# Last expert layer of a fused two-block kernel: gathers, weight places and the overflow count arranged anew

## The chip, the cores and the metric

The kernel runs on one core of a Trainium2 chip. Its time is the device time of one execution in microseconds (us), and the median of several executions is given. One of them is recorded by the hardware profiler; all rows below come from that execution. PE is the matrix engine (TensorE), DVE the vector engine, ACT the scalar engine, SP the engine whose queue issues all the large weight transfers here.

## The reference

Two transformer blocks run one after the other on 256 tokens of 1024 numbers, in float32. The last part of the second block is a mixture of eight experts; each token goes to two of them:

```python
def _moe_swiglu(h, w_router, w_gate, w_up, w_down):
    logits = (h @ w_router).astype(jnp.float32)
    top_vals, top_idx = lax.top_k(logits, TOP_K)
    top_w = jax.nn.softmax(top_vals, axis=-1)
    gates = jnp.sum(jax.nn.one_hot(top_idx, N_EXPERTS, dtype=jnp.float32) * top_w[..., None], axis=-2)
    out = jnp.zeros_like(h)
    for e in range(N_EXPERTS):
        y = _swiglu(h, w_gate[e], w_up[e], w_down[e])
        out = out + gates[..., e:e + 1].astype(h.dtype) * y
    return out
```

`_swiglu` is silu(h W_gate) times (h W_up), multiplied by W_down. The inner width FF is 3584, so each expert has three matrices of 1024 x 3584 numbers, 44 MB, and all eight are read from memory: 352 MB. `h` is the RMS-normalised residual; the block adds `out` to it.

## The kernel before, in words

`moe2` is the last stage of the program, from about 1107 us to the end. It works on routed tokens only.

- **Choice.** `logits` (L685) transposes the residual x, multiplies it by the router, and picks two experts for each token. It also splits all of x into two parts, `th` (ACT, L300) and `tl` (DVE, L137), each in fp32r, a rounded float32 form. A number is then the sum of its two parts.
- **Places.** The experts are ranked by how many tokens they have. Place 0 is expert 0; the rest follow by count. Places 0 to 4 are large, with 128 slots for tokens, 5 to 7 small, with 64. They run in the order `SEQ = (0, 5, 1, 2, 6, 3, 4, 7)`. A token beyond an expert's slots is an overflow: `beyond` (L723) counts those, with a chain on DVE, a transpose on PE (L735) and a read of the number by SP (L928), after which a second pass runs if the number is not zero.
- **Gathers.** The tokens of an expert are brought together by a product with a one-hot matrix. `gather(p, k)` does this for one of eight blocks of 128 rows: four fp32r products, `th` and `tl` times two halves of the tokens, then ACT and DVE split the result. `gather_small` does it for all three small experts at once, 192 columns wide. The eight gathers of place 0 stand ahead of everything; `some()` sets the others, one behind each step of a down product of the expert ahead: the small gathers in place 0, those of 1 in 5, of 2 in 1, of 3 in 6, of 4 in 3.
- **Weights.** Each expert has 42 weights of 1 MB: 28 for gate and up, in seven chunks of 512 columns (the loop over `c`), and 14 for down. In a large expert `slab` (L266) loads a weight into one of five `raw` tiles (DMA at L270). ACT copies each half of it to fp32r (L277) and DVE subtracts (L137); the two parts go to one of seven `wx` tiles. Three products per block follow (`mm3`): six records of 512 columns for each half of a weight. In a small expert `whole` (L261) loads the weight (L1456 gate and up, L1592 down) and PE uses it in plain float32, without splitting. It takes the five `raw` and then the seven `wx` tiles in rotation, by a counter that runs through the whole program.
- **Order.** PE follows the written order in this stage (`manual_schedule`). The other engines are ordered by the scheduler. SP issues the weight transfers one after the other, and each waits there until its tile is free.
- The work on the tables by places (`by_place`, `one_hot`, the shares) and the overflow count stand in the loop at `p == 0 and c == 1`; in chunk 2 each expert multiplies its slots by the gate.

Of the kernel before, what the change touches and what calls it, by code (L numbers as in the profile page):

```python
# [19 lines left out]
P = 128  # L20
D = 1024
# [32 lines left out]
    "moe2": dict(t8=3, t4=0, t2=5, t1=3, t0=4, tz=16, hh=7, hl=7),  # L54
# [15 lines left out]
class Fused:  # L70
    def __init__(self, ctx, tc, A):
# [7 lines left out]
        self.fences, self.holds, self.wholes = [], [], -1  # L79
# [181 lines left out]
    def whole(self, *shape):  # L261

        n, self.wholes = sum(WBUFS.values()), self.wholes + 1
        tag = "raw" if self.wholes % n < WBUFS["raw"] else "wx"
        return self.wp.tile([P, *shape], F32, name=self.name("whole"), tag=tag, bufs=WBUFS[tag])

    def slab(self, src, k, n):
        nc = self.nc
        raw = self.wp.tile([P, k, n], F32, name=self.name("raw"), tag="raw", bufs=WBUFS["raw"])
# [415 lines left out]
    def logits(self, x, w, choose, bias=None):  # L685

        th, tl = self.T([P, 2, D], F32R), self.T([P, 2, D], F32R)
# [3 lines left out]
        def half(t, c):  # L691
            self.split(th[:, t, c:c + 512], tl[:, t, c:c + 512], x[:, t, c:c + 512])
# [671 lines left out]
    def moe2(self, x, out):  # L1364
# [5 lines left out]
        names = "l1_moe_w_gate_2", "l1_moe_w_up_2", "l1_moe_w_down_2"  # L1370
        lg, rank, chosen = self.T([P, 2, 8]), self.T([P, 2, 8]), self.T([P, 2, 8], BF)
# [5 lines left out]
        raw, th, tl = self.logits(x, self.rt2_w, choose)  # L1377
# [28 lines left out]
        def gather(p, k):  # L1406
# [6 lines left out]
            for i, q in enumerate((th, tl)):  # L1413
                for t in range(2):
                    self.mm(ps, q[:, t, k * P:(k + 1) * P], oh[:, t, p], i == 0 and t == 0, i == 1 and t == 1)
# [5 lines left out]
        def gather_small(p, k):  # L1421
# [4 lines left out]
            for i, q in enumerate((th, tl)):  # L1426
                for t in range(2):
                    self.mm(ps, q[:, t, k * P:(k + 1) * P], oh[:, t, p:E, 0:CAP1], i == 0 and t == 0, i == 1 and t == 1)
# [74 lines left out]
        for at, p in enumerate(SEQ):  # L1503
            hids, small = [], p >= SMALL
            first, final = at == 0, at == E - 1
            ahead = SEQ[at + 1] if not final else p
            ahead = iter([] if final or ahead > SMALL else
                         [(gather_small if ahead == SMALL else gather, (ahead, k)) for k in range(8)])

            def some():  # L1510
                for f, args in ahead:
                    f(*args)
                    break
# [8 lines left out]
            for c in range(FF // 512):  # L1522
                hid = self.T([P, 512])
                if small:
# [3 lines left out]
                    later.append((turn_small, (hid, hids)))  # L1528
                else:
# [8 lines left out]
                if p == 0 and c == 1:  # L1538
# [37 lines left out]
                    over, cnt = self.beyond(slot, shares, None, E)  # L1576
# [116 lines left out]
```

## Time and profile before

| | before |
|---|---|
| median of 3 runs | 2085.85 us (2085.8 to 2087.02) |
| profiled execution | 2086.38 us, span 2084.6 us |
| granted TensorE clock, mean | 0.987 |
| PE busy | 1980.3 us (95%) |
| DVE busy | 1201.8 us (58%) |
| ACT busy | 989.9 us (47%) |
| moved by DMA | 576.46 MB, mean 277 GB/s |

The span is what the recorded instructions cover; the execution's own time is 1.8 us longer. Busy shares are means over the whole program, which has several stages; the last one is about 47% of it. A window row shows the time from and to, its length, then for PE, PEld (weight loads), DVE, ACT and POOL the busy time with the number of instructions, then the granted clock (1.00 is 2.4 GHz), the busy share of the DMA engines and the GB/s that they moved. In a timeline a row is a start, a length and an instruction, or several alike in a row; behind it in brackets stands the idle time before it and what ended that. A wait on a "DMA" is one for a transfer to land.

### The profile page before, as it was taken

To read this page: it belongs to the slowest core of one execution; us is meant where nothing else is said; L and a number is where in the kernel's file an instruction comes from. 1 tells how busy PE (TensorE), PEld (TensorE's weight loads), DVE (VectorE), ACT (ScalarE), POOL (GpSimd) and SP (SyncE) were. 2 spreads that over 40 slices of the span, in tenths; PEclk is the share of its full clock that TensorE was granted. 3 is DMA by queue.
4 is the path that set the end of the run, shared out by engine and by line. 5 is a ranking of instruction groups with operands and counts; after the bars stand their busy time and mean duration, and the time that the engine had idled before them with its cause. 6 is when DMAs were issued, how large, how long until landed. Compare 5 with 4: busy or idle time off the path is not lost. (4 is left out here: it accounts for less than half of the span.)

```text
span 2084.6 us, 27119 instructions
## 1 busy us (share of the span) xinstructions
PE 1980.3 (95%) x10288; PEld 1411.8 (68%) x10288; DVE 1201.8 (58%) x1853; ACT 989.9 (47%) x1469; POOL 42.4 (2%) x66
## 2 busy tenths in 40 slices
PE   7999998999989999999998999899999889999987
PEld 7977445875437979987776883378877237887722
DVE  6856116643146656656778860189886018988600
ACT  4564123632236444444566861177675117767510
POOL 2000000000000000000000000000000000000000
PEclk9999998999999999999999999999999999999999
DMA  9337995547976446555335999999999999999998
GB/s 265 125 104 243 331 368 187 181 154 272 366 285 227 142 142 202 183 168 198 122 117 204 319 351 386 402 348 353 342 349 332 387 402 371 358 342 342 376 387 330
DMA packets 327411, 576.46 MB, mean 277 GB/s; under 512 B 11738, under 2 KB 124088, under 8 KB 327144
## 3 DMA queue, kind: packets, MB, share of 16 engines
q1 hardware_dynamic: 324808, 568.33, 78.1%
q0 software_dynamic: 2464, 6.31, 1.1%
q8 instruction: 83, 1.36, 0.3%
q14 instruction: 56, 0.46, 0.1%
HBM read 573.55 MB, written 1.05 MB: 276 GB/s over the span
## 5 line engine op out<-in xcount | busy, mean ns | idle before, releaser
L137 DVE TENSOR_TENSOR wx<-raw,wx 128x1024 fp32r<-128x1024 f32 (+3 forms) x642 | 752.7, 1210 | 172.9 <-ACT wx L277 167.2
L277 ACT CAST wx<-raw 128x1024 fp32r<-128x1024 f32 (+3 forms) x642 | 641.0, 1043 | 202.2 <-PE acc L149 144.2
L149 PE MATMUL ms<-wx,hl 128*128 128x512 f32 x1960 | 515.7, 396 | 5.0 <-ACT wx L277 2.7
L149 PEld LDWEIGHTS ms<-wx,hl 128*128 128x128 f32 x1960 | 364.6, 189 | 93.2 <-DVE wx L137 14.4
L149 PE MATMUL acc<-hl,wx 128*128 128x256 f32 x2112 | 273.5, 288 | 2.7 <-ACT wx L277 1.6
L149 PEld LDWEIGHTS acc<-hl,wx 128*128 128x128 f32 x2112 | 261.8, 194 | 5.7 <-ACT wx L277 2.1
L149 PE MATMUL ms<-whole,xg 128*64 128x512 f32 x672 | 177.4, 600 | 24.7 <-DMA whole<-in_l_moe_w_up_dram 24.6
L134 ACT ACTIVATE t<-ms,tz 128x512 f32<-128x512 f32 (+4 forms) x101 | 60.5, 602 | 290.8 <-PE ms L149 281.6
L149 PE MATMUL acc<-wx,hl 128*128 128x512 f32 (+1 forms) x720 | 180.3, 403 | 4.7 <-DVE wx L137 3.1
L149 PE MATMUL ms<-wx,hh 128*128 128x512 f32 x560 | 176.4, 395 | 1.5 <-DVE wx L137 1.5
L146 DVE SCALAR_TENSOR_TENSOR t<-ms,tz,t 128x512 f32<-128x512 f32 (+2 forms) x69 | 51.8, 750 | 214.6 <-ACT t L134 174.8
L149 PE MATMUL acc<-wx,t 128*128 128x512 f32 (+1 forms) x732 | 174.0, 394 | 0.5 <-DVE t L1038 0.5
L149 PEld LDWEIGHTS acc<-wx,hl 128*128 128x128 f32 x720 | 135.1, 193 | 35.7 <-DVE wx L137 3.6
L149 PEld LDWEIGHTS acc<-wx,t 128*128 128x128 f32 x732 | 135.2, 188 | 29.9 <-DVE t L1038 0.9
L149 PEld LDWEIGHTS ms<-whole,xg 128*64 128x64 f32 x672 | 52.2, 136 | 128.4 <-issue 73.2
L149 PEld LDWEIGHTS ms<-wx,hh 128*128 128x128 f32 x560 | 103.5, 188 | 25.0 <-DVE wx L137 3.8
L149 PE MATMUL ms<-whole,hl 128*64 128x512 f32 x512 | 117.0, 598 | 0.5 <-DVE t L137 0.5
L149 PE MATMUL ms<-whole,hh 128*64 128x512 f32 x336 | 83.5, 604 | 12.4 <-DMA whole<-in_l_moe_w_down_dram 12.3
L149 PEld LDWEIGHTS tp<-t,t 128*128 128x128 f32 (+1 forms) x432 | 57.3, 185 | 49.5 <-issue 32.4
L146 DVE SCALAR_TENSOR_TENSOR t<-tp,tz,t 128x512 fp32r<-128x512 f32 x32 | 23.9, 747 | 95.5 <-ACT t L134 95.5
L149 PEld LDWEIGHTS ms<-whole,hl 128*64 128x64 f32 x512 | 35.0, 136 | 60.1 <-issue 55.8
L149 PE MATMUL tp<-t,t 128*128 128x256 f32 (+4 forms) x432 | 72.1, 294 | 1.6 <-DVE t L137 1.6
(275 smaller groups left out, 1544.4 us busy)
## 6 DMA issues: line engine op xcount, KB each, us to landing
raw<-in_l_moe_w_gate_dram SPq DMA_DIRECT2D x70, 1024.0 KB, 7.2
raw<-in_l_moe_w_up_dram SPq DMA_DIRECT2D x70, 1024.0 KB, 7.2
raw<-in_l_moe_w_down_dram SPq DMA_DIRECT2D x70, 1024.0 KB, 7.6
whole<-in_l_moe_w_gate_dram SPq DMA_DIRECT2D x42, 1024.0 KB, 14.1
whole<-in_l_moe_w_up_dram SPq DMA_DIRECT2D x42, 1024.0 KB, 14.2
whole<-in_l_moe_w_down_dram SPq DMA_DIRECT2D x42, 1024.0 KB, 18.3
whole<-in_moe_w_gate_dram SPq DMA_DIRECT2D x64, 512.0 KB, 8.2
whole<-in_moe_w_up_dram SPq DMA_DIRECT2D x64, 512.0 KB, 8.8
```

Source lines behind the costliest of these rows:

```text
L134: return self.nc.scalar.activation(out, in_, func, **kw)
L137: return self.nc.vector.tensor_tensor(out, a, b, op=op)
L146: return self.nc.vector.scalar_tensor_tensor(out, a, s, b, op0=op0, op1=op1, **kw)
L149: return self.nc.tensor.matmul(out, lhsT, rhs, start=start, stop=stop, **kw)
L277: nc.scalar.copy(h, raw[:, a:a + m])
```

## The change

Four things change in `moe2`:

- The two parts `th`, `tl` of x are not made; gathers multiply plain float32 x by the one-hot matrix, two products in place of four.
- The two tiles that this sets free become places for weights (`more=2`). `slab` rotates over seven tiles instead of five, `whole` over fourteen (five, two, seven) instead of twelve, and both counters start anew at this layer.
- The gathers are spread differently: those of places 1 and 2 lie in the small expert 5, those of 3 and 4 in 6, from the sixth chunk on and then behind each down step; the small gathers stay in place 0; the large experts 1 to 4 have none.
- `beyond` stands at chunk 4 of place 0 instead of chunk 1.

```diff
--- before.py
+++ after.py
@@ -51,7 +51,7 @@
     "sg": dict(t8=6, t4=2, t2=4, t1=1, t0=3, tz=8),
     "ffn": dict(t8=7, t4=0, t2=4, t1=1, t0=1, tz=16),
     "diff": dict(t8=0, t4=7, t2=8, t1=4, t0=8, tz=24, hd=8, acc=3, av=1),
-    "moe2": dict(t8=3, t4=0, t2=5, t1=3, t0=4, tz=16, hh=7, hl=7),
+    "moe2": dict(t8=1, t4=0, t2=5, t1=3, t0=4, tz=16, hh=7, hl=7, more=2),
 }
 
 
@@ -76,7 +76,7 @@
         self.wp = ctx.enter_context(tc.tile_pool(name="weights", bufs=1))
         self.hp = ctx.enter_context(tc.tile_pool(name="inputs", bufs=1))
         self.n = 0
-        self.fences, self.holds, self.wholes = [], [], -1
+        self.fences, self.holds, self.wholes, self.raws = [], [], -1, -1
         self.x = self.X()
         for t in range(2):
             self.nc.sync.dma_start(self.x[:, t], A["x"][0, t * P:(t + 1) * P])
@@ -260,13 +260,24 @@
 
     def whole(self, *shape):
 
-        n, self.wholes = sum(WBUFS.values()), self.wholes + 1
-        tag = "raw" if self.wholes % n < WBUFS["raw"] else "wx"
-        return self.wp.tile([P, *shape], F32, name=self.name("whole"), tag=tag, bufs=WBUFS[tag])
+        more = self.bufs.get("more", 0)
+        n, self.wholes = sum(WBUFS.values()) + more, self.wholes + 1
+        if self.wholes % n < WBUFS["raw"]:
+            tag = "raw"
+        else:
+            tag = "more" if self.wholes % n < WBUFS["raw"] + more else "wx"
+        return self.piece("whole", [P, *shape], tag)
+
+    def piece(self, name, shape, tag):
+        if tag == "more":
+            return self.ap.tile(shape, F32, name=self.name(name), tag=tag, bufs=self.bufs[tag])
+        return self.wp.tile(shape, F32, name=self.name(name), tag=tag, bufs=WBUFS[tag])
 
     def slab(self, src, k, n):
         nc = self.nc
-        raw = self.wp.tile([P, k, n], F32, name=self.name("raw"), tag="raw", bufs=WBUFS["raw"])
+        self.raws += 1
+        at = self.raws % (WBUFS["raw"] + self.bufs.get("more", 0))
+        raw = self.piece("raw", [P, k, n], "raw" if at < WBUFS["raw"] else "more")
         nc.sync.dma_start(raw, src)
         m = k // SPLIT if k % SPLIT == 0 else k
         hs, ls = [], []
@@ -682,14 +693,15 @@
             at += w.shape[1]
         return wc
 
-    def logits(self, x, w, choose, bias=None):
-
-        th, tl = self.T([P, 2, D], F32R), self.T([P, 2, D], F32R)
+    def logits(self, x, w, choose, bias=None, parts=True):
+
+        th, tl = (self.T([P, 2, D], F32R) if parts else None for _ in range(2))
         n = w.shape[2]
         out, xT = self.T([P, 2, n]), self.HL([P, 8, S], F32)
 
         def half(t, c):
-            self.split(th[:, t, c:c + 512], tl[:, t, c:c + 512], x[:, t, c:c + 512])
+            if parts:
+                self.split(th[:, t, c:c + 512], tl[:, t, c:c + 512], x[:, t, c:c + 512])
 
         for t in range(2):
             s = slice(t * P, (t + 1) * P)
@@ -1368,13 +1380,14 @@
         nc, A = self.nc, self.A
         E, FF = 8, 3584
         names = "l1_moe_w_gate_2", "l1_moe_w_up_2", "l1_moe_w_down_2"
+        self.wholes = self.raws = -1
         lg, rank, chosen = self.T([P, 2, 8]), self.T([P, 2, 8]), self.T([P, 2, 8], BF)
 
         def choose(t, lg):
             self.ranks(rank[:, t:t + 1], lg[:, None], 1, 8)
             self.ts(chosen[:, t], rank[:, t], 1.5, None, OP.is_lt)
 
-        raw, th, tl = self.logits(x, self.rt2_w, choose)
+        raw, _, _ = self.logits(x, self.rt2_w, choose, parts=False)
         rx = self.token_scale(x)
         found, slot = self.places(chosen, E, True), self.T([P, 2, E])
         oh = self.T([P, 2, E, CAP2], F32R)
@@ -1410,9 +1423,8 @@
                 inputs[p] = xp[:, 0], xp[:, 1]
             xH, xL = inputs[p]
             ps = self.PS([P, CAP2], "ms" if p == 0 and k % 2 else "tp")
-            for i, q in enumerate((th, tl)):
-                for t in range(2):
-                    self.mm(ps, q[:, t, k * P:(k + 1) * P], oh[:, t, p], i == 0 and t == 0, i == 1 and t == 1)
+            for t in range(2):
+                self.mm(ps, x[:, t, k * P:(k + 1) * P], ohf[:, t, p], t == 0, t == 1)
             last = self.split(xH[:, k], xL[:, k], ps, self.gcol("l1_moe", k))
             if p == 0:
                 self.awake(psr[3], WG)
@@ -1423,9 +1435,8 @@
             if k == 0:
                 inputs[p] = self.xp.tile([P, 8, E - p, CAP1], F32, name=self.name("xg"), tag="x")
             ps = self.PS([P, E - p, CAP1], "tp")
-            for i, q in enumerate((th, tl)):
-                for t in range(2):
-                    self.mm(ps, q[:, t, k * P:(k + 1) * P], oh[:, t, p:E, 0:CAP1], i == 0 and t == 0, i == 1 and t == 1)
+            for t in range(2):
+                self.mm(ps, x[:, t, k * P:(k + 1) * P], ohf[:, t, p:E, 0:CAP1], t == 0, t == 1)
             self.act(inputs[p][:, k], ps, AF.Copy, scale=self.gcol("l1_moe", k))
 
         def source(p, i, k0, nk, c0, n):
@@ -1503,9 +1514,8 @@
         for at, p in enumerate(SEQ):
             hids, small = [], p >= SMALL
             first, final = at == 0, at == E - 1
-            ahead = SEQ[at + 1] if not final else p
-            ahead = iter([] if final or ahead > SMALL else
-                         [(gather_small if ahead == SMALL else gather, (ahead, k)) for k in range(8)])
+            after = [q for q in SEQ[at + 1:at + 3] if q < SMALL] if small else SEQ[at + 1:at + 2] if first else []
+            ahead = iter([(gather_small if q == SMALL else gather, (q, k)) for q in after for k in range(8)])
 
             def some():
                 for f, args in ahead:
@@ -1526,6 +1536,8 @@
                     self.act(hid[64:128], ps[0:64], AF.Silu, scale=scol[0:64])
                     self.stt(hid[64:128], ps[64:128], scol[64:128], hid[64:128], OP.mult, OP.mult)
                     later.append((turn_small, (hid, hids)))
+                    if c > 4:
+                        some()
                 else:
                     g = up(p, c, 0)
                     catch_up()
@@ -1573,7 +1585,9 @@
                     self.ts(room, place[:, 0], SMALL - 0.5, float(CAP2 - CAP1), OP.is_lt, OP.mult)
                     self.ts(room, room, 1000.0 + CAP1 - 0.5, None, OP.add)
                     self.tt(slot, slot, room[:, None].to_broadcast([P, 2, E]), OP.subtract)
-                    over, cnt = self.beyond(slot, shares, None, E)
+                    spare = slot, shares
+                if p == 0 and c == 4:
+                    over, cnt = self.beyond(*spare, None, E)
                 if c == 2:
                     psg = self.PS([P, 1], "tp")
                     for t in range(2):
```

On PE, in expert 0, the transpose of the count (L735, after L747) stands between weights. Before, where `ms_10100` is the up product of chunk 1, `wx` are halves of weights and `hl` the gathered tokens:

```order
L149 MATMUL ms_10100<-wx_10123,hl_9901 128x512 x6
L149 MATMUL ms_10100<-wx_10126,hl_9901 128x512 x6
L735 MATMUL ms_10190<-c_78,tz_10188 1x128
L149 MATMUL ms_10197<-wx_10200,hl_9901 128x512 x6
L149 MATMUL ms_10197<-wx_10203,hl_9901 128x512 x6
L149 MATMUL ms_10197<-wx_10221,hl_9901 128x512 x6
L149 MATMUL ms_10197<-wx_10224,hl_9901 128x512 x6
L1468 MATMUL tp_10239<-c_78,t_1713_10047 128x128 x4
```

In the changed kernel, in the up product of chunk 4 and what follows:

```order
L149 MATMUL ms_10411<-wx_10434,hl_9891 128x512 x6
L149 MATMUL ms_10411<-wx_10437,hl_9891 128x512 x6
L747 MATMUL ms_10456<-c_78,tz_10454 1x128
L149 MATMUL ms_10463<-wx_10466,hl_9891 128x512 x6
L149 MATMUL ms_10463<-wx_10469,hl_9891 128x512 x6
L149 MATMUL ms_10463<-wx_10487,hl_9891 128x512 x6
L149 MATMUL ms_10463<-wx_10490,hl_9891 128x512 x6
L1479 MATMUL tp_10505<-c_78,t_1785_10358 128x128 x4
```

The transpose has moved down by twelve weights; before it stood ahead of chunk 2, now it stands ahead of chunk 5.

On SP, the first weights of the second small expert, place 6, and what each waits for. Before:

```order
L1456 DMA whole_13489<-in_l_moe_w_gate_dram 128x4x512 [waits DVE_49,PE_49]
...
L1456 DMA whole_13491<-in_l_moe_w_up_dram 128x4x512 [waits DVE_49,PE_49]
...
L1456 DMA whole_13501<-in_l_moe_w_gate_dram 128x4x512 [waits DVE_49,PE_49]
...
L1456 DMA whole_13503<-in_l_moe_w_up_dram 128x4x512 [waits DMAHW6_49,DVE_49,PE_49]
...
L1456 DMA whole_13521<-in_l_moe_w_gate_dram 128x4x512 [waits DMAHW7_49,DVE_49,PE_49]
...
L1456 DMA whole_13523<-in_l_moe_w_up_dram 128x4x512 [waits DMAHW0_49,DVE_49,PE_49]
```

In the changed kernel (the rows between them are register instructions):

```order
L1467 DMA whole_13415<-in_l_moe_w_gate_dram 128x4x512 [waits DMAHW4_49,DVE_49]
...
L1467 DMA whole_13417<-in_l_moe_w_up_dram 128x4x512 [waits DMAHW5_49,DVE_49]
...
L1467 DMA whole_13427<-in_l_moe_w_gate_dram 128x4x512 [waits DMAHW6_49,DVE_49]
...
L1467 DMA whole_13429<-in_l_moe_w_up_dram 128x4x512 [waits DMAHW7_49,DVE_49]
...
L1467 DMA whole_13447<-in_l_moe_w_gate_dram 128x4x512 [waits DMAHW0_49,DVE_49]
...
L1467 DMA whole_13449<-in_l_moe_w_up_dram 128x4x512 [waits DMAHW1_49,DVE_49]
```

Before, the first transfers go to tiles that PE has to leave; now they go to tiles that DVE has to leave.

On PE, in the small expert of place 5, the changed kernel has a gather between chunks 5 and 6, where `x_9633` is the residual itself:

```order
L149 MATMUL ms_11185<-whole_11198,xg_10672 64x512
L149 MATMUL ms_11185<-whole_11200,xg_10672 64x512
L149 MATMUL tp_11220<-t_1679_9861,x_9633 128x128 x2
L149 MATMUL ms_11226<-whole_11227,xg_10672 64x512
L149 MATMUL ms_11226<-whole_11229,xg_10672 64x512
```

It is two products of the program; before, a gather was four.

## Rows read from the trace of the kernel before

**Rows 1.** Windows by expert, places 0, 5, 1, 2, 3, 4; columns as named above
```profile
1115.20:1247.90 132.70, 125.33 (x580) 103.63 (x579) 110.26 (x128) 94.74 (x106) 0.00 (x0) 0.97 0.92 325
1247.90:1350.10 102.20, 93.08 (x410) 31.82 (x410) 9.17 (x18) 11.37 (x24) 0.00 (x0) 1.00 1.04 395
1350.10:1482.40 132.30, 129.63 (x590) 104.20 (x590) 113.83 (x113) 97.40 (x114) 0.00 (x0) 0.99 1.01 357
1482.40:1606.50 124.10, 123.53 (x551) 99.15 (x550) 104.13 (x99) 86.16 (x98) 0.00 (x0) 1.00 0.94 330
...
1716.30:1847.20 130.90, 128.24 (x590) 103.04 (x590) 113.89 (x113) 97.78 (x114) 0.00 (x0) 1.00 1.02 369
1847.20:1971.20 124.00, 123.44 (x551) 99.15 (x551) 104.13 (x99) 86.01 (x98) 0.00 (x0) 1.00 0.97 345
```

**Rows 2.** Waits of PE from 1080 us: total, times, longest
```profile
PE ms L149 <- DMA whole<-in_l_moe_w_up_dram: 24.6, 28, 1.6
PE ms L149 <- DMA whole<-in_l_moe_w_down_dram: 12.3, 21, 0.7
```

**Rows 3.** Windows at the second small expert's start and in the first's down
```profile
1592.00:1612.00 20.00, 20.00 (x89) 14.64 (x88) 10.61 (x11) 7.26 (x8) 0.00 (x0) 1.00 0.80 286
1612.00:1632.00 20.00, 15.99 (x66) 4.88 (x65) 1.51 (x2) 1.73 (x3) 0.00 (x0) 1.00 1.05 387
...
1320.00:1340.00 20.00, 19.59 (x94) 7.53 (x92) 2.46 (x7) 2.57 (x7) 0.00 (x0) 1.00 1.03 409
```

**Rows 4.** Timeline of PE in expert 0: start, length, instruction, idle before
```profile
1132.02 5.70 PE L149 MATMUL ms<-wx,hl 128*128 128x512 f32 x24
1145.09 0.37 PE L735 MATMUL ms<-c,tz 128*1 128x128 f32 x1 [7.37 <-DVE tz L733]
1145.11 7.15 PE L149 MATMUL ms<-wx,hl 128*128 128x512 f32 x24
```

**Rows 5.** Timeline of DVE in expert 0: the reduction that makes the gate
```profile
1143.87 0.29 DVE L1549 TENSOR_REDUCE tz<-t 128x16 f32<-128x128 f32 x1
```

**Rows 6.** Window around that stall; the column after POOL is the granted clock
```profile
1140.00:1150.00 10.00, 4.92 (x16) 4.02 (x17) 5.99 (x16) 1.46 (x2) 0.00 (x0) 0.66 0.73 272
```

**Rows 7.** Timeline of DVE at the layer's start, between logits and choice
```profile
1108.25 0.68 DVE L137 TENSOR_TENSOR t<-x,t 128x512 fp32r<-128x512 f32 x1
```

**Rows 8.** Timelines of PE: gathers at the start, the small gather, down steps
```profile
1111.68 0.61 PE L149 MATMUL ms<-t,t 128*128 128x128 f32 x4
1112.13 0.61 PE L149 MATMUL tp<-t,t 128*128 128x128 f32 x4
...
1213.77 0.59 PE L149 MATMUL tp<-t,t 128*128 128x192 f32 x4
1214.19 0.65 PE L149 MATMUL ms<-wx,hh 128*128 128x512 f32 x2
...
1320.95 1.94 PE L149 MATMUL ms<-whole,hh 128*64 128x512 f32 x8
1322.82 0.66 PE L149 MATMUL tp<-t,t 128*128 128x128 f32 x4
1323.41 1.94 PE L149 MATMUL ms<-whole,hh 128*64 128x512 f32 x8
```

**Rows 9.** Timeline of PE in the attention: plain float32 products
```profile
1077.72 1.58 PE L149 MATMUL av<-t,t 128*128 128x128 f32 x12
```

**Rows 10.** Windows of the down half, places 1 and 2
```profile
1437.90:1482.40 44.50, 44.13 (x213) 36.52 (x212) 38.96 (x41) 32.22 (x40) 0.00 (x0) 1.00 1.02 367
1565.60:1606.50 40.90, 40.52 (x180) 32.76 (x178) 33.03 (x30) 25.21 (x28) 0.00 (x0) 1.00 0.91 317
```

**Rows 11.** Timeline of SP's queue at the second small expert's first weights
```profile
1598.23 0.37 SPq L1456 DMA_DIRECT2D whole<-in_l_moe_w_gate_dram  x1
1599.61 0.37 SPq L1456 DMA_DIRECT2D whole<-in_l_moe_w_up_dram  x1
```

**Rows 12.** DMA issues from 1150 us: count, KB each, us from issue to landing
```profile
whole<-in_l_moe_w_gate_dram SPq DMA_DIRECT2D x42, 1024.0 KB, 14.1
```

## Prediction

> **What bounds the kernel now.** I read the stretches by expert first [rows 1]. The last layer works through eight experts by place: 0 large, 5 small, 1 and 2 large, 6 small, 3 and 4 large, 7 small. In a large expert PE is busy nearly throughout (129.63 of 132.30 us in the one at place 1, 123.53 of 124.10 at place 2), while the weights arrive at 325 to 369 GB/s. In the small one at place 5 PE is busy 93.08 of 102.20 us and the weights arrive at 395 GB/s. The waits of PE say the same from the other side [rows 2]: in this layer PE waits 24.6 + 12.3 us for weights that a small expert uses as they land, and hardly for anything else. So the limit alternates. A large expert takes as long as PE's work, and the DMA queue has time over; a small one takes as long as its weights need to land, counted from how many were already in the buffers when it began. A saturated small expert lands a weight of 1.0486 MB every 2.71 us in gate and up (387 GB/s) and every 2.56 us in down (409 GB/s) [rows 3].
>
> One exception is inside the large expert 0: PE stands for 7.37 us before the transpose of the overflow count, which waits for a reduction on DVE [rows 4].
>
> **Expert 0.** The transpose moves from behind weight 7 to behind weight 19 in PE's program, so the 7.4 us go, if nothing else is late at once. Next in PE's order is the gate product after weight 11. DVE makes its operand at 1143.87 + 0.29 us [rows 5]; PE, which now starts weight 8 at 1145.09 and would start it when the 24 records at 1132.02 end [rows 4], near 1137.7, needs it four weights of 2.85 us (half of those 5.70) later, near 1149. That leaves some 4 us. What stays of the count on DVE now follows at weight 19, with no long chain ahead of it.
> The stall costs twice: in the 10 us around it the granted clock was 0.66 [rows 6], a mean between the full 2.4 GHz and half of it, after PE had stood; the first 24 records afterwards took 7.15 us where 24 before took 5.70 [rows 4]. That returns 1.45.
> At the start DVE's split of x stands for 0.6 between the logits and the choice [rows 7]; it is left out: -0.6.
> A gather is now two plain float32 products in place of four split ones. The trace has no plain gather. Below, it could cost no more than the present 0.45 us (128 columns) or 0.42 (192) [rows 8]; it is not cheaper, since no fewer records than now are to be expected. Above, the nearest rows are the plain products of the attention before: six products of 128 columns are 12 records in 1.58 us [rows 9], so two records and at most 0.26 each, 0.53 for a gather. At 192 columns I scale the small experts' plain products: the down step's eight records of 512 columns stand 1.87 us ahead of the next start, with two column halves side by side [rows 8], so 0.47 per record alone, so 0.175 at 192 and 0.70 for four records. I take the upper values, because they come from plain products: 8 x 0.08 = +0.6 at the start, 8 x 0.28 = +2.2 for the small gather in expert 0's down, all on PE's path. Both ends stay in the range.
> Expert 0: -7.4 - 1.45 - 0.6 + 0.6 + 2.2 = **-6.6**.
>
> **Gathers out of the large experts.** The down half of place 1, with eight gathers, takes 44.5 us; that of place 2, with none, 40.9 [rows 10]. Places 1 and 3 now carry none: 3.5 each, **-7.0**. They move into the small experts 5 and 6, 16 in each: two beside gate and up, 14 beside down. There a step with a gather takes 2.46 us of PE [rows 8] and 2.54 with a plain one, against 2.56 for its weight, so they are hidden, barely; without that cover each would cost up to 0.5. Two of the steps come after the last weight's landing in part: +0.4 in each expert, **+0.8**. PE's order is written by hand, so behind a gather only the next step's products queue.
>
> **Fourteen places.** A small expert's weights go to all places, 12 before and 14 now; a large one's to the raw tiles, five before and seven now. In a large expert the queue waits for places (DVE's subtraction frees a raw tile), not for bandwidth, as its GB/s show. Two more places put two more transfers ahead when the small expert begins: 2 x 2.71 = 5.4 us at each of three switches, **-16.2**. It holds only if the queue has that much time over. From 387 GB/s the slack is 21 us at place 0, 10 + 18 at places 1 and 2, 6 + 14 at 3 and 4 [rows 1]; the shorter large experts take 6.6, 3.5 and 3.5 of it, the two places 5.4, which leaves 10 or more.
> At the second switch the order matters as well. The counter of places runs on from the first small expert, and 42 weights leave it in the middle of 12: the second small expert begins on the converted tiles, each of which PE must leave first. The queue issues its first weight at 1598.23 us and then one per 1.38 us, PE's pace [rows 11], and the window around it moves 286 GB/s where 387 passes after it [rows 3]: 20 x (1 - 286/387) = 5.2 us of the queue stand idle. With 42 = 3 x 14 and the counter set to -1 it begins on raw tiles, which wait for DVE, well ahead of PE. **-5.2**.
> The first use of the two new tiles waits for the attention's space and is issued behind later weights; those two are wanted 25 us into PE's list of expert 0, so I cost it at nothing. The reads of the experts' numbers move to one before each expert, and the read of the count behind all weights: the queue of SP then has nothing of DVE's late chain in its way. Nothing, where the lead of expert 0 covers it.
>
> **The sum.** -6.6 - 7.0 + 0.8 - 16.2 - 5.2 = -34.2 against the profiled execution of 2086.4 (span 2084.6), so 2052.2. The median of the runs, 2085.85, lies 0.5 lower: **2051.5 us**.
>
> **Rivals.**
> *The places do not carry (0.17).* The conversions on ACT and DVE may hold the queue's lead, whatever the places: DVE is busy 113.83 of 132.30 us at place 1 [rows 1]. Then -16.2 falls away: -18.0, about 2068. Against it: the transfers wait for a free raw tile, and that is what is added.
> *The stall moves (0.1).* In expert 0 DVE is still behind, and PE waits at the gate product or for a conversion: the -8.9 of stall and clock is lost, 2060. For it: the margin is about 4 us only.
> *Plain products cost as much as four split ones each (0.05).* Eight of the present 0.111 us are 0.89 for a gather: +3.6 at the start and +3.4 for the small gather instead of +2.8 together, and each of 28 down steps would take 2.46 + 0.45 = 2.91 against 2.56: +9.8. Together 14 more, 2065.5. Against it stand two records per plain product [rows 9].
> The Trainium skill, FP8 and Floating Point Precision, section TensorE Precision Notes, says that true float32 takes four passes through the array. By that page the time would come out near this rival's 2065.5; the two records that this trace shows per plain product do not bear it out, though what one record does inside it cannot be seen.
> *Transfers in flight share the engines (0.03), slower.* With more places, more transfers are under way. If the first of seven lands with the last instead of ahead of it, it comes 6 x 2.7 = 16 us late wherever PE has run dry, at the switches into and out of small experts, five in all: 5 x 16 - 34 = +46, 2132. From three such switches on the sign turns. Against it: a weight in a small expert takes 14.1 us from issue to landing [rows 12], yet PE's longest wait for one is 1.6 [rows 2], so they land one behind the other at 2.7.
> The Trainium skill, DMA: Bandwidth & Descriptors, section Queues, rings and completion order, states that completion is not first in, first out per issuing engine. Taken to its end that is this rival; the waits of at most 1.6 us show little of it in this kernel.
> *The change does not do what it says (0.03).* The new tiles could come free so late that the queue stands in expert 0 and the gain is used up there: within 4 us of before.
>
> **How the numbers follow.** The forecast has 0.62. Its own range, down by 2.8 if a gather costs what it did and by 8.1 if the places carry three transfers a switch, up by 8.1 if they carry one, is 2041 to 2060. The stall that moves, the plain products at four and the places that do not carry end at 2060 to 2068, so 2041 to 2068 leaves out under 2 in 10. Two per mille, 4.2 us, is what a measurement can tell from no change: faster 0.93 (forecast and three rivals, with a little off for their tails), same 0.03, slower 0.04.
>
> **What would show it.** No idle time over 1 us before the transpose of the count, and a granted clock of 0.9 or more there. Down halves near 41 us at places 1 and 3. The small experts at places 5 and 6 near 97 and 99 us instead of 102 and 110, the second with no window under 370 GB/s around its start. Issue to landing in the small experts near 19 us instead of 14, at unchanged landings 2.7 apart. Gathers as four records of about 0.13. It would be wrong if the large experts' GB/s did not rise, if PE's waits for weights in the small experts stayed at 37 us or grew, or if a new wait for DVE stood in expert 0.

## Result and the profile after

| | before | changed |
|---|---|---|
| median | 2086.06 us (2085.8 to 2087.02, 4 runs) | 2054.54 us (2052.17 to 2058.99, 4 runs) |
| ratio, 95% interval | | 0.985 [0.9836, 0.9863] |
| profiled execution, span | 2086.38, 2084.6 | 2056.82, 2055.1 |
| granted clock, mean | 0.987 | 0.987 |

The forecast was 2051.5 with a range of 2041 to 2068. Windows by expert of the changed kernel, in the order in which the experts run (places 0, 5, 1, 2, 6, 3, 4, 7), columns as in [rows 1]:

```profile
1116.20:1243.00 126.80, 125.85 (x581) 104.41 (x581) 108.96 (x128) 94.75 (x107) 0.00 (x0) 1.00 0.96 341
1243.00:1339.00 96.00, 95.11 (x445) 35.08 (x444) 11.63 (x25) 14.61 (x33) 0.00 (x0) 1.00 1.04 395
1339.00:1467.30 128.30, 125.93 (x556) 100.29 (x555) 108.94 (x104) 91.29 (x104) 0.00 (x0) 0.99 1.03 376
1467.30:1591.80 124.50, 123.86 (x552) 99.16 (x552) 106.40 (x101) 87.72 (x100) 0.00 (x0) 1.00 1.00 355
1591.80:1693.70 101.90, 96.95 (x442) 35.17 (x442) 11.63 (x25) 14.35 (x32) 0.00 (x0) 1.00 1.04 395
1693.70:1822.30 128.60, 126.22 (x559) 100.53 (x558) 108.94 (x104) 91.58 (x105) 0.00 (x0) 0.99 1.03 374
1822.30:1946.80 124.50, 123.87 (x553) 99.21 (x552) 106.40 (x101) 87.77 (x100) 0.00 (x0) 1.00 1.00 354
1946.80:2046.40 99.60, 86.61 (x376) 27.07 (x375) 6.36 (x10) 8.35 (x17) 0.00 (x0) 1.00 1.00 378
```

Against [rows 1]: expert 0 takes 6 us less, its clock is 1.00 in place of 0.97, and every large expert draws its weights faster (341, 376, 355, 374, 354 GB/s in place of 325, 357, 330, 369, 345). That is where the queue's idle time went. In the expert at place 5 PE is busy for 95.11 of the 96.00 us, where it had been 93.08 of 102.20, and the weights still arrive at 395 GB/s: that small expert now keeps both near their limit. The waits of PE of the changed kernel, from 1080 us on:

```profile
PE ms L149 <- DMA whole<-in_l_moe_w_up_dram: 11.6, 15, 1.6
PE ms L149 <- DMA whole<-in_l_moe_w_down_dram: 6.8, 11, 0.7
...
PE ms L149 <- DVE tz L749: 1.0, 1, 1.0
```

The waits for weights have halved, from the 24.6 and 12.3 of [rows 2] to 11.6 and 6.8. The 7.4 before the transpose of the count [rows 4] is gone. A wait of 1.0 is new: PE's timeline in expert 0 shows it behind the transpose.

```profile
1173.39 0.27 PE L747 MATMUL ms<-c,tz 128*1 128x128 f32 x1
1174.62 1.67 PE L149 MATMUL ms<-wx,hl 128*128 128x512 f32 x6 [0.95 <-DVE tz L749]
```

DVE's timeline says why:

```profile
1169.75 4.62 DVE L137 TENSOR_TENSOR wx<-raw,wx 128x1024 fp32r<-128x1024 f32 x4
1174.29 0.27 DVE L749 TENSOR_REDUCE tz<-ms 1x1 f32<-1x128 f32 x1
```

The transpose now gets its operand in time, but the DVE instruction that reads its result stands behind four conversions, and the next product of PE waits for that bank.

The gathers, at the start, inside expert 0 and inside a small expert's down, from PE's timeline of the changed kernel:

```profile
1112.78 0.61 PE L149 MATMUL ms<-t,x 128*128 128x128 f32 x4
1113.22 0.61 PE L149 MATMUL tp<-t,x 128*128 128x128 f32 x4
...
1204.15 0.81 PE L149 MATMUL tp<-t,x 128*128 128x192 f32 x4
1204.67 0.77 PE L149 MATMUL ms<-wx,hh 128*128 128x512 f32 x2
...
1331.25 1.94 PE L149 MATMUL ms<-whole,hh 128*64 128x512 f32 x8
1333.12 0.71 PE L149 MATMUL tp<-t,x 128*128 128x128 f32 x4
1333.76 1.94 PE L149 MATMUL ms<-whole,hh 128*64 128x512 f32 x8
```

A plain gather is four records as before, since each of its two products makes two. At 128 columns it takes 0.44 at the start, like the split one [rows 8]; at 192 columns 0.52 to 0.64 to the next start in place of 0.42; a down step with a gather is 2.51 in place of 2.46. The down half of place 1, without gathers, is as long as that of place 2 was [rows 10]:

```profile
1426.30:1467.30 41.00, 40.63 (x181) 32.82 (x179) 34.17 (x31) 26.94 (x30) 0.00 (x0) 1.00 1.00 361
```

The DMA issues of the changed kernel from 1150 us on, which the prediction had expected near 19 us instead of the 14.1 of [rows 12]:

```profile
whole<-in_l_moe_w_gate_dram SPq DMA_DIRECT2D x42, 1024.0 KB, 14.1
...
whole<-in_l_moe_w_down_dram SPq DMA_DIRECT2D x42, 1024.0 KB, 18.2
```

Nothing moved there. So the places do not work as the prediction put it, although the small experts did become shorter. Runs 5 to 7 settle that.

### The profile page after: what moved, and what is told of

Same layout as the page of the kernel before. It is cut to its first block, busy times and chain, and to the rows that moved or that the text cites. A ratio compares the mean times of both kernels' runs of the same rounds, so it can differ in the third digit from the quotient of the medians.

```text
span 2055.1 us, 27128 instructions
## 1 busy us (share of the span) xinstructions
PE 1976.2 (96%) x10288; PEld 1411.4 (69%) x10288; DVE 1198.1 (58%) x1849; ACT 985.0 (48%) x1465; POOL 42.5 (2%) x66
## 3 DMA queue, kind: packets, MB, share of 16 engines
HBM read 573.55 MB, written 1.05 MB: 280 GB/s over the span
## 5 line engine op out<-in xcount | busy, mean ns | idle before, releaser
L149 PE MATMUL ms<-whole,xg 128*64 128x512 f32 x672 | 166.3, 598 | 11.9 <-DMA whole<-in_l_moe_w_up_dram 11.6
L134 ACT ACTIVATE hl<-tp,c 128x128 fp32r<-128x128 f32 x84 | 29.7, 366 | 87.2 <-PE tp L149 60.9
L146 DVE SCALAR_TENSOR_TENSOR hl<-tp,c,hl 128x128 fp32r<-128x128 f32 x84 | 28.3, 348 | 66.1 <-ACT hl L134 65.4
## 6 DMA issues: line engine op xcount, KB each, us to landing
whole<-in_l_moe_w_gate_dram SPq DMA_DIRECT2D x42, 1024.0 KB, 14.1
whole<-in_l_moe_w_up_dram SPq DMA_DIRECT2D x42, 1024.0 KB, 14.2
whole<-in_l_moe_w_down_dram SPq DMA_DIRECT2D x42, 1024.0 KB, 18.2
```

Source lines behind the costliest of these rows:

```text
L134: return self.nc.scalar.activation(out, in_, func, **kw)
L146: return self.nc.vector.scalar_tensor_tensor(out, a, s, b, op0=op0, op1=op1, **kw)
L149: return self.nc.tensor.matmul(out, lhsT, rhs, start=start, stop=stop, **kw)
```

## Experiments

Every length below is the time from PE's first product of one expert to its first product of the next (of place 7: to the end of its last), read as starts from PE's timeline of one profiled execution each. "Layer" is their sum. Times beside them are medians. The kernel before ran again beside each group of runs, with 2087.29 beside runs 1 to 4, 2086.82 beside 5 to 8 and 2086.64 beside 9 to 11; the ratios are to these, and medians of different groups compare to one or two microseconds.

| us | 0 | 5 | 1 | 2 | 6 | 3 | 4 | 7 | layer | median |
|---|---|---|---|---|---|---|---|---|---|---|
| before | 132.9 | 103.8 | 130.5 | 124.3 | 111.4 | 129.1 | 124.2 | 104.4 | 960.6 | 2086.06 |
| changed | 126.9 | 97.1 | 127.1 | 124.6 | 103.2 | 127.2 | 124.5 | 99.4 | 930.0 | 2054.54 |
| 1 count late alone | 125.1 | 101.1 | 129.1 | 124.2 | 111.3 | 129.0 | 124.2 | 105.1 | 949.1 | 2076.96 |
| 2 twelve places | 126.7 | 102.9 | 125.7 | 124.7 | 113.4 | 127.2 | 124.7 | 105.0 | 950.1 | 2075.54 |
| 3 twelve, from raw | 126.7 | 105.6 | 127.2 | 124.6 | 107.7 | 127.1 | 124.6 | 104.7 | 948.1 | 2071.89 |
| 4 gathers back | 126.9 | 95.7 | 131.0 | 124.5 | 101.6 | 129.4 | 124.6 | 99.1 | 932.8 | 2059.3 |
| 5 raw 7, whole 12 | 126.9 | 99.7 | 126.9 | 124.6 | 102.6 | 127.3 | 124.7 | 99.3 | 932.0 | 2056.76 |
| 6 raw 5, whole 14 | 126.7 | 102.5 | 125.6 | 124.7 | 107.6 | 125.7 | 124.7 | 105.0 | 942.3 | 2070.72 |
| 7 thirteen | 126.9 | 99.9 | 125.5 | 124.6 | 105.5 | 125.7 | 124.7 | 102.9 | 935.6 | 2060.31 |
| 8 earlier gathers | 127.5 | 95.7 | 126.9 | 124.6 | 101.5 | 125.6 | 124.6 | 98.9 | 925.3 | 2051.46 |
| 9 changed again | 126.9 | 97.3 | 125.6 | 124.7 | 102.2 | 125.6 | 124.7 | 98.7 | 925.6 | 2052.32 |
| 10 gathers alone | 126.9 | 95.7 | 128.3 | 124.7 | 101.5 | 126.9 | 124.6 | 99.1 | 927.5 | 2053.28 |
| 11 count in place 5 | 125.5 | 95.6 | 128.5 | 124.7 | 101.2 | 127.1 | 124.6 | 99.9 | 927.1 | 2054.92 |

**1. The count alone.** In the kernel before, `beyond` moves from chunk 1 to chunk 4:

```diff
-                    over, cnt = self.beyond(slot, shares, None, E)
+                    spare = slot, shares
+                if p == 0 and c == 4:
+                    over, cnt = self.beyond(*spare, None, E)
```

> The kernel before with the count alone moved from chunk 1 to chunk 4 of place 0. Theory: the 7.4 us of PE's stall and 1.4 of slow clock behind it go, about 1 us comes back as the wait for the count in chunk 4 that the changed kernel shows (0.95), and the rest of the layer keeps its times, since each expert after it starts that much earlier: about 2078. Rival: without the lighter start of the changed kernel DVE is still behind, and the wait moves to the gate product of chunk 2 or to a conversion; then PE has a wait of several us between 1135 and 1160 and the time stays above 2083.

2076.96, ratio 0.9955 [0.9938, 0.9971]. Expert 0 is 7.8 us shorter, and the stall goes to no other place of it. PE's timeline shows a wait of 0.73 behind the transpose:

```profile
1172.13 0.27 PE L735 MATMUL ms<-c,tz 128*1 128x128 f32 x1
1173.14 3.04 PE L149 MATMUL ms<-wx,hl 128*128 128x512 f32 x12 [0.73 <-DVE t L146]
```

The prediction's rival of a stall that moves is out, and the 7.4 + 1.45 less a wait of its own are shown. The layer lost more than that: 2.7 at place 5, the length of one transfer, by which this place differs between runs 2 and 3 as well, and 1.4 at place 1, where the granted clock of the first 10 us was 0.83 in the profile before and 1.00 in this one (see run 9).

**2 and 3. Twelve places, in the old order and from the raw tiles.** The changed kernel with

```diff
-    "moe2": dict(... hh=7, hl=7, more=2),
+    "moe2": dict(... hh=7, hl=7, more=0),
```

and for the second of the two also

```diff
             hids, small = [], p >= SMALL
+            if small:
+                self.wholes = -1
```

> The changed kernel with twelve places for weights in place of fourteen (five raw for the large experts), everything else as changed; 42 weights again end in the middle of the rotation. Theory of the places: 16 us come back from two transfers less at each of three switches and 5 from the second small expert's start on converted tiles, so about 2075 against 2054. The first weight of each small expert lands about 5 us later against PE's first use of it, 10 at the second. Rival: what the small experts gained came from the shorter large experts and the stall that went, which leave the queue more time; then the time stays within 4 us of the changed kernel.

> Twelve places, but each small expert begins its rotation on the raw tiles. Theory: the order of places is worth 5 us at the second small expert (place 6) alone, so about 2070, and place 6 is as long as place 5 within 2 us. Rival: the order was worth nothing beside the number of places, and the time is that of the twelve places in their old order.

2075.54, 0.9941 [0.9925, 0.9958], and 2071.89, 0.9922 [0.9902, 0.9942]. Without the two tiles 21 us come back. The order alone shortens place 6 from 113.4 to 107.7: 5.7, where 5.2 had been worked out of the idle queue in [rows 3]. The large expert ahead of it, place 2, shows the idle queue that goes, in run 2 and then in run 3:

```profile
1472.80:1597.40 124.60, 124.01 (x551) 99.27 (x551) 106.47 (x101) 88.05 (x100) 0.00 (x0) 1.00 0.96 339
1475.40:1600.00 124.60, 123.93 (x552) 99.22 (x551) 106.41 (x101) 88.34 (x100) 0.00 (x0) 1.00 1.00 353
```

Place 5, which the order does not touch, differs by 2.7 between the two profiles: at its start five weights had landed in run 2 and four in run 3. So one expert's length is good to about one transfer, and the medians' 3.7, whose intervals overlap, agree with the 5.7 within it. The tiles alone, from run 3 to the changed kernel, give 17.4 in the median.

**4. The gathers where they were.**

```diff
-            after = [q for q in SEQ[at + 1:at + 3] if q < SMALL] if small else SEQ[at + 1:at + 2] if first else []
+            after = [q for q in SEQ[at + 1:at + 2] if q <= SMALL]
...
-                    if c > 4:
-                        some()
```

> The changed kernel, fourteen places and all, with the gathers spread as before: those of place 2 inside place 1, of 4 inside 3, of 1 inside 5 and of 3 inside 6, one behind each down step. Theory: the down halves of places 1 and 3 are 3.5 us longer again, the small experts 5 and 6 end 1.4 us earlier each, because 8 of their down steps lose a gather and PE catches up with the landings: plus 4 in all, about 2058. Rival A: with fourteen places the large experts have no slack left, and all 7 us come back. Rival B: the small experts pay as much as the large ones gain, and nothing changes.

2059.3, 0.9873 [0.9854, 0.9892]: 4.8 above the changed kernel. Place 1 is 3.8 longer (place 3 is 2.2 longer, and 3.8 against run 9, where the clock did not fall at its start either); the window of the down half of place 1 is

```profile
1422.20:1466.90 44.70, 44.33 (x212) 36.56 (x211) 36.82 (x39) 29.52 (x38) 0.00 (x0) 1.00 0.99 345
```

against the 41.00 above. The small experts 5 and 6 are 1.3 and 1.6 shorter. So the gathers' move is worth its 3.5 per large expert, less some 1.4 in each small one: 14 down steps of 2.51 under landings of 2.56 catch up so slowly that PE, 2.0 us behind the landings at the second of these steps, is still 1.46 behind the last one (place 6 of the changed kernel: landed at 1689.76, used from 1691.22; in this run it is 0.52).

**5 and 6. Whose places carry.** In run 5 only the large experts use the new tiles, in run 6 only the small ones:

```diff
-        more = self.bufs.get("more", 0)
+        more = 0
```

(with the restart of run 3), and

```diff
-        at = self.raws % (WBUFS["raw"] + self.bufs.get("more", 0))
+        at = self.raws % WBUFS["raw"]
```

> The changed kernel, but only the large experts use the two new tiles (seven raw); the small experts rotate over twelve places, each beginning on the raw tiles. Theory: what carries is how far the queue runs ahead while a large expert computes, so the raw tiles of the large experts do it; once a small expert runs, the queue itself is full (an issue takes SP 2.4 us there, and issue to landing stays at 14 us with twelve or fourteen places). Then 2054 to 2057. Rival: the small experts' own places carry, as they take the transfers at the switch; then about 2070, as with twelve places for all.

> The mirror: the large experts rotate over five raw tiles as before, the small experts over all fourteen places. Theory: the two tiles are filled only after the five raw ones have been, when the queue is nearly full already, so little of the 16 us is left: about 2068 (2065 to 2072). Rival: the places of the small experts carry; then 2054 to 2057.

2056.76, 0.9851 [0.9835, 0.9868], and 2070.72, 0.9918 [0.9902, 0.9935]. The large experts' raw tiles carry it; the small experts' own places give 1.2 us with five raw tiles (run 3 to run 6) and 2.2 with seven (run 5 to the changed kernel), less than these medians can tell. SP's queue at place 6 shows how. With seven raw tiles (run 5), then PE's first use:

```profile
1573.93 0.37 SPq L1467 DMA_DIRECT2D whole<-in_l_moe_w_gate_dram  x1
```

```profile
1595.67 0.65 PE L149 MATMUL ms<-whole,xg 128*64 128x512 f32 x2
```

The first weight is issued 21.7 us ahead of its use. With five raw tiles and fourteen places (run 6):

```profile
1583.04 0.37 SPq L1467 DMA_DIRECT2D whole<-in_l_moe_w_gate_dram  x1
...
1592.70 0.37 SPq L1467 DMA_DIRECT2D whole<-in_l_moe_w_up_dram  x1
1593.28 1.43 SPq L1467 DMA_DIRECT2D whole<-in_l_moe_w_gate_dram  x1
1594.90 2.43 SPq L1467 DMA_DIRECT2D whole<-in_l_moe_w_up_dram  x1
```

```profile
1597.12 1.08 PE L149 MATMUL ms<-whole,xg 128*64 128x512 f32 x4
```

14.1 us ahead, as in run 3 with twelve places. The sixth and seventh weight go to the free tiles at once, 0.58 apart, but the seventh issue takes SP 1.43 us, though its tile is as free as the sixth's, and those from the eighth on 2.4 instead of 0.37. I read that as a full queue, which takes the next transfer only when one leaves; the unchanged 14.1 us to landing agrees. Then more places behind it change nothing, and the lead has to be made before, while the large expert computes. The landings in the same traces show that there it is one transfer per raw tile: when PE starts place 7, three weights have landed with five raw tiles (runs 3 and 6), four with six (run 7) and five with seven (run 5 and the changed kernel).

**7. Thirteen places.** `more=1`, with the restart of run 3.

> One new tile in place of two for all experts (six raw, thirteen places), each small expert beginning on the raw tiles. Theory: each place is worth one transfer of 2.7 us at each of the three switches, so the time lies half way between twelve from raw (2071.9) and fourteen (2054.5): about 2063, and at the start of the small experts one more weight has landed than with twelve. Rival: the gain comes with a threshold (all of it from the first tile, or none before the second): within 3 us of one of the ends.

2060.31, 0.9869 [0.9852, 0.9885]. It lies between the ends, with 11.6 us from the first tile and 5.8 from the second (8.0 by run 9); half and half would have been 8.7 each. The first weight of place 6 is issued 16.3 us ahead of its use. There is no threshold, and whether the first tile is worth more than the second the spreads of some 3 us leave open.

**8, 10 and 11. The remaining lag and the remaining wait.** Earlier gathers (8, 10 and 11) and the count in chunk 6 (8), or in the second chunk of place 5 (11):

```diff
-                    if c > 4:
+                    if c > 1:
...
-                if p == 0 and c == 4:
+                if at == 1 and c == 1:
```

> The changed kernel with the gathers inside the small experts 5 and 6 beginning with chunk 2 in place of chunk 5 (five beside gate and up, eleven beside down), and the count in chunk 6 in place of 4. Theory: PE's lag of 1.45 us behind the last landing of each of these experts goes, as gate and up leave PE idle between weights and the last three down steps have no gather, and the wait of 0.95 for the count shrinks or goes: 2 to 4 us less than the changed kernel, about 2051. Rival: the lag is made at the head of the down product and not by its gathers, or the wait for the count follows it; then no difference.

> Only the earlier gathers of the run before (from chunk 2 in the small experts 5 and 6), the count in chunk 4. Theory: PE's lag of 1.45 at the end of both experts goes, and expert 0 stays at 126.9 us, since the count's move to chunk 6 had made its wait longer (1.6 in place of 0.95): 2.5 to 4 us under the changed kernel. Rival: the lag comes back, as it was the count's place that changed what follows.

> The earlier gathers, and the count in the second chunk of the small expert at place 5, where PE waits for weights and DVE has next to no conversions (9 us busy in 102 before). Theory: the wait for the count in expert 0 goes (0.95) and none takes its place, so expert 0 takes 126 us: 1 us under the kernel with the gathers alone, 3.5 to 5 under the changed kernel. Rival: the transpose there waits for the reduction on DVE behind the first conversions of the next large expert, and PE stands as long in expert 5 as it did in expert 0.

Medians of 2051.46 (0.9836 [0.9818, 0.9855]), 2053.28 (0.9834 [0.9822, 0.9847]) and 2054.92 (0.9845 [0.9833, 0.9858]); the changed kernel in the rounds of the last two had 2052.32 (0.9839 [0.9826, 0.9852]). All four are the same as far as these can tell. Locally each edit did what was expected: places 5 and 6 are 0.7 to 2.0 shorter than in the two profiles of the changed kernel, and expert 0 is 1.4 shorter when the count leaves it (with the count in chunk 6 it is 0.6 longer: the wait grew to 1.6). But the 2 to 5 us that had been expected of them did not come: the large experts behind took longer again, place 1 in runs 10 and 11 by 2.7 and 2.9 against run 9. PE's timeline at the end of place 5 in run 10:

```profile
1333.95 1.94 PE L149 MATMUL ms<-whole,hh 128*64 128x512 f32 x8
1335.81 0.61 PE L149 MATMUL tp<-tz,t 128*128 128x1 f32 x4
1337.82 0.72 PE L149 MATMUL ms<-wx,hl 128*128 128x512 f32 x1 [1.40 <-ACT wx L288]
1339.08 8.14 PE L149 MATMUL ms<-wx,hl 128*128 128x512 f32 x23 [0.54 <-DVE wx L137]
```

and the window there:

```profile
1337.00:1347.00 10.00, 8.64 (x24) 6.38 (x24) 7.49 (x7) 5.70 (x6) 0.00 (x0) 0.66 1.05 386
```

PE now reaches the large expert's first product sooner and waits there for ACT and DVE to convert a weight that has only just landed (at 1336.62). These two waits are hardly longer together than in the changed kernel (1.40 + 0.54 against 1.05 + 0.76, run 9). What gives the gain back is the clock behind them: the 23 records take 8.14 us, against 5.55 without a fall (run 9). Where it did not fall, at place 3 of run 8, the large expert took 125.6, as in run 9, in spite of the earlier gathers. The clock of 0.66 stands in both of runs 10 and 11, and at place 1 only; run 8, with the same gathers, has 0.83 there. Whether the earlier gathers make the deeper fall likelier, two profiles don't tell. No version faster than the changed kernel was found.

**9. The changed kernel again**, for the spread.

> The changed kernel once more, in the same rounds as the two below. Theory: its time varies by 5 us and more from one execution to the next because the clock falls at different places of the program in each (in the first profile at 780, 980 and 1690 us, one of them in a stage that nothing was changed in); its median stays within 3 us of 2054.5, and the last layer, from the first product to the last, keeps 930 us within 3. Rival: the spread lies in the last layer's queue, and that length varies as much as the whole.

2052.32 (2051.12 to 2055.82); the layer took 925.6, 4.4 less than in the first profile, so the layer does not keep its length within 3, and the first part of the theory holds only in part. Windows at two of the switches from a small to a large expert, first profile:

```profile
1340.00:1350.00 10.00, 8.99 (x33) 6.56 (x34) 7.13 (x8) 6.28 (x8) 0.00 (x0) 0.83 1.05 387
1690.00:1700.00 10.00, 8.19 (x35) 4.97 (x32) 6.17 (x9) 7.12 (x9) 0.00 (x0) 0.87 1.05 386
```

and in this run:

```profile
1340.00:1350.00 10.00, 9.28 (x43) 7.09 (x44) 8.38 (x8) 7.84 (x10) 0.00 (x0) 1.00 1.05 387
1690.00:1700.00 10.00, 8.19 (x41) 6.16 (x42) 7.89 (x9) 8.01 (x10) 0.00 (x0) 1.00 1.05 386
```

The first large product behind place 5 in the first profile, and in this run:

```profile
1340.24 0.50 PE L149 MATMUL ms<-wx,hl 128*128 128x512 f32 x1 [1.05 <-ACT wx L288]
1341.51 7.12 PE L149 MATMUL ms<-wx,hl 128*128 128x512 f32 x23 [0.76 <-DVE wx L137]
```

```profile
1339.46 0.50 PE L149 MATMUL ms<-wx,hl 128*128 128x512 f32 x1 [1.05 <-ACT wx L288]
1340.72 5.55 PE L149 MATMUL ms<-wx,hl 128*128 128x512 f32 x23 [0.76 <-DVE wx L137]
```

The same instructions with the same waits ran once under a fallen clock and once not. Places 1 and 3 differ by 1.5 and 1.6 with it. The same reading, in the 10 us from 1 us ahead of the first product, sorts these lengths in every profile of the table whose large experts carry no gathers: 125.5 to 125.7 us at a clock of 1.00, 126.9 to 127.3 at 0.83, 128.3 and 128.5 at 0.66. So differences of 1.4 or 2.8 between two rows at places 1 and 3 are the clock's. Of the rest 1.0 and 0.7 lie in places 6 and 7, whose weights took 111.0 and 110.3 us from the first landing to the last in the first profile and 109.7 and 109.2 in this run: that part is the rival, a spread of the transfers. The start of the layer differs too (1116.27 and 1115.29), from windows at 780 and 980 us, in stages that the change does not touch.

## Why the prediction was right, and where not

The time was 3 above the forecast in the first four runs and 1 above in the second five, inside the range both times. Term by term, the first profile against the profile before:

- **Expert 0: -6.6 forecast.** The layer's start to the first gather is 0.4 shorter, from the first gather to expert 5's first product it is 6.1 (1112.33 to 1243.17 against 1111.18 to 1248.15): 6.5. The stall and its clock went as costed (run 1). Entries that were off cancelled: the gathers of 128 columns cost nothing more (+0.6 forecast), and 0.95 of new wait was not foreseen. The step that failed there: "what stays of the count on DVE now follows at weight 19, with no long chain ahead of it". There is no long chain, but four conversions are enough. A new wait for DVE in expert 0 was one of the prediction's signs of being wrong; it came, at 0.95 against the 7.4 that went. The small gathers added about 0.2 each, 1.6 in all (2.2 forecast).
- **Gathers out of the large experts: -7.0 and +0.8.** The down halves fell by 3.5 to 3.7 (44.5 to 41.0, and 44.7 to 41.0 in run 4). The last gathers in the small experts cost 1.4 each in place of 0.4. "Hidden, barely" was right in the middle of the down product; at its head PE begins late and, at 2.51 against 2.56 a step, makes it up by 0.05 a step only. A cover is worth its difference to the work, not its length.
- **Fourteen places: -16.2.** Measured between run 3 and the changed kernel 17.4, so the size was right, and so were the "two more transfers ahead" (five weights landed at the start of place 7 in place of three). The carrier was right only in half. The prediction counted the places of the small experts (12 and 14) and the raw tiles of the large ones (five and seven) as one, and drew "issue to landing in the small experts near 19 us" from the former: it stayed at 14.1, and run 6 shows that the small experts' places alone give next to nothing. By the issue times the queue is full by itself in a small expert; the large experts' raw tiles set how far ahead it is when one begins. The check of the slack was needed and held: with the tiles in use the large experts at places 1 and 2 drew 376 and 355 GB/s, still under 387, which leaves 14 us over the two. (Of its "10 or more", place 0 has only 9: 21 less 6.6 and 5.4.)
- **The order at the second small expert: -5.2.** 5.7 (runs 2 and 3). All the same, place 6 took 101.9 us where the prediction's signs had 99. Between the two first profiles its first landing moved from 3.4 to 13.2 us ahead of PE's first use, 9.8 of the 10.6 costed for tiles and order together, and the larger lag at its end took another 1.0.
- **Rivals.** "The places do not carry" is what run 6 shows for the small experts; for the large ones it fell. The stall did not move (run 1). Plain products at four times the cost are out at these sizes: two records per product, 0.11 each at 128 columns, so a plain product took twice a split one. The Trainium skill, FP8 and Floating Point Precision, section TensorE Precision Notes, has four passes for true float32. No run here shows what happens inside a record, but at 512 columns the trace comes near the four. A small expert's plain records start in pairs 0.43 us apart (1314.17 and 1314.60 in the changed kernel), which I read as one record for each of two column halves. With two records to a product that makes 0.86, against 0.23 for one fp32r product of 512 columns (72 records from 1116.27 to 1132.72). So the prediction's "do not bear it out" is a reading of 128 columns alone: there the gathers got off cheaply because a split record took 0.11 too, half of what one of 512 columns takes. Transfers that share the engines did not show: with fourteen places PE's longest wait for a weight stayed 1.6, and in every run the recorded landings of the small experts' weights come in the order of their issue. The Trainium skill, DMA: Bandwidth & Descriptors, section Queues, rings and completion order, allows completions out of order. None was seen among these landings.

The sum of the forecast, -34.2, lies beside -29.6 in the first pair of profiles and -34.3 in the medians of run 9's rounds (2086.64 to 2052.32). Of the 4.6 between the forecast and the first profile 1.5 stand ahead of the layer, in stages that the change leaves alone (its first transpose starts at 1105.29 instead of 1103.77). 2.0 are the larger lag of the last gathers, and 1.6 a fallen clock at place 3, where the kernel before had none; some 0.5 the rest gave back. That run 9 comes within 0.1 of the sum is in part luck: the larger lag stands against 1.2 more than costed from the tiles and 0.5 from the order, and the clock's falls differ from one execution to the next. (From the median of 2085.85 the sum gives 2051.7; the 2051.5 is a slip of 0.2.)

## What to carry to other kernels

Where a stage limited by an engine hands over to one limited by transfers, look first at the buffers of the first: here they decided how far the queue was ahead at the handover, and each was worth one transfer per handover. Further buffers in the second did next to nothing; the time that an issue itself takes was the hint that the queue was full there. Work moved under a cover only a few hundredths of a microsecond longer than itself was hidden in the middle but showed at the ends. An instruction moved out of one wait should be followed to the one that must read its result.

## What the runs showed of the hardware

- An issue of a 1 MB transfer took SP 0.37 us at the start of a small expert and 2.4 from the eighth on, near the 2.7 from landing to landing (run 6). Read as a full queue, it holds some 14 us of transfers of gate and up, and some 18 of down; twelve, thirteen or fourteen tiles made no difference to that (14.1 to 14.2 and 18.2 to 18.3 in runs 3, 5, 6 and 7).
- A plain float32 product of 128 columns is two records and took as long as two fp32r products (0.44 for a gather either way); at 192 columns its records start 0.16 apart against 0.11, and at 512 columns a plain product takes an estimated 0.86 against 0.23 (two records, starting 0.43 apart).
- After a small expert, behind PE's waits of 1.05 and 0.76 us for the first conversions, the granted clock at the switch was 0.83 in one execution and 1.00 in another of the same program (the chip's two levels are 1.2 and 2.4 GHz). 0.83 went with some 1.5 us, and 0.66, in two other runs, with some 2.8. What decides it stays open.
